# A two-layer diffusion step on one core: the fourth feed-forward row by seven products, three output splits placed later, and a projection's weights made ahead of modulation tiles

## The chip, the core and the metric

The program runs on one core of a Trainium2 chip. The metric is the device time of one execution in microseconds (us). Three runs of the kernel before gave 1493.72, 1493.82 and 1495.14 us, so the median is 1493.82 us.

The core's engines run side by side, each through its own list of instructions in order: TensorE (PE in the profile; PEld is its weight load), VectorE (DVE), ScalarE (ACT), GpSimd (POOL) and SyncE (SP), which in this kernel issues nearly all DMAs. An instruction that waits holds up everything behind it on its engine.

## The reference, cut to what matters

Two groups of tokens go through the same two trunk layers: 512 latent tokens and 128 prompt tokens. They are held together as T = 640 columns of feature-major tiles (128 features by 640 tokens, eight tiles for the model width 1024).

```python
for l in range(DEPTH):                                    # DEPTH = 2
    sh1, sc1, g1, sh2, sc2, g2 = ada_modulation(cond, w_mod[l], b_mod[l])
    h = modulate(rms_norm(x, norm_mix[l]), sh1, sc1)
    # l = 0: 8 latent-attention (MLA) heads and 8 neighbourhood heads, joined, then @ w_out_a
    # l = 1: grouped-query attention, then @ w_out_c
    x = x + g1 * mixer(h)
    h = modulate(rms_norm(x, norm_ffn[l]), sh2, sc2)
    x = x + g2 * swiglu(h, w_ffn_in[l], w_ffn_out[l])
def swiglu(h, w_in, w_out):
    gate, up = jnp.split(h @ w_in, 2, axis=-1)            # 1024 -> 2 x 2816
    return (jax.nn.silu(gate) * up) @ w_out
```

Everything is in 32-bit floats, and the products keep that precision by splitting each operand into a high and a low part and taking three matmuls (high x high, high x low, low x high).

## The kernel before

**Splits.** `rsplit(src, name)` (lines 458 to 463) writes the high part of a 128 x 640 tile with an ACT copy (L461) and the low part with a DVE subtraction (L462). `unit(src, n, name)` (lines 168 to 175) does the same for a 128 x 1024 tile of weights: a load into one of three `raw` buffers (SP, L165), an ACT copy (L173) and a subtraction (L174, on DVE, or on POOL for a few) into one of three `w` buffers of the pool `wp`.

**The order.** The framework takes the program's text as priority, simulates the engines with a cost model and writes out a fixed order for every engine; buffers are given out in that order too, so a load waits until the instructions on the buffer's last content have ended. `after(inst, fn)` binds the instructions of `fn` that run on the engine of `inst` behind `inst`; it adds no wait across engines.

**Latent attention of layer 0.** Eight heads in a loop; `exps[h, j]` is the ACT exponential of head h and query block j (L965, tile `mp`), and POOL then scales the block by the inverse sum (L384). A head's tail (five groups of four transposes `mt`, their splits `mts`, and the products `mo` with the values) is woven into the next head's scores. Beside it, the eight finished output tiles are split for the projection that follows: `oN[0..3]` from the neighbourhood heads, done before the loop, and `oM[0..3]`, one for each pair of latent heads. The splits of `oN` are bound behind `exps[h, 3]` of heads 0, 2, 4 and 5. Those of `oM[0..2]` stand after the loop in the text and are bound to nothing, so the planner takes them up as gaps appear. `oM[3]` needs the last head. All these splits lie in eight pairs of ring buffers.

**Projection of layer 0** (`mixer_out`, name `oa`). For each of eight output rows n it takes the weights `un(n)` (tile `oaw`n) and 24 matmuls for each half of the columns, in the order oN0 to oN3, oM0 to oM3; rows 0 and 1 leave their last part (oM3) to the end of row 1. `evac` adds the result to x (`xr`, L324), which `x_again` has loaded afresh behind a DVE copy out of `oMs3l` (L1672). Between the rows stands `beside(n - 1)`: with the counts (1, 1, 1, 1, 0, 0, 0) it loads one 128 x 1024 tile `wm` of the modulation weights (L1648) and takes two DVE products with accumulation (L1630, tile `junk`). The weights are asked for by the first matmul that needs them, so in the text `beside(n - 1)` stands ahead of `un(n)`; with `early` set, `un(n)` stands ahead. The projection of layer 1 has `early` set.

**Feed-forward of layer 0** (`ffn`, l = 0). Each of the 22 rows (`fb`) of 128 hidden features takes a tile of gate weights and a tile of up weights. The first `FEW[0]` = 4 rows are plain: 2 tiles x 2 halves x 8 steps x 3 matmuls. The rows after them take seven products over half-size blocks instead of eight (`seven`, lines 1169 to 1186, in the manner of Strassen and Winograd): DVE forms sums of quarters of the two weight tiles (`s13`, `s24`: L1179 to L1184), three 1024-wide tiles wX, wY, wZ are split by `split` (L1370 on ACT, L1371 on DVE), and the 512-wide wW by L1176 and L1177. On the other side stand sums of the normalised tokens (`h01D`, `h01N`, `h01C`, `h01E`), made by `add_up` during the plain rows 0 and 1. After each row, `hidden` splits the result (`hd`) and sends it out to DRAM; `step("fb", fb)` may take modulation tiles.

`split` counts its calls in `turn[0]` and gives its results to the pool `fp` and `wp` in turn. The same counter goes on into the second half, the projection back to 1024 features: `wout` adds one for each of its calls and, for a call with a single tile, takes the buffers of `rawp` and `wp` when the count is odd, and those of the pool `fo` (one raw buffer, two `w` buffers) when it is even. `rawp` is shared with the loads of modulation tiles. The tiles are `wo_`; the first figure is the output row, the second the first of its blocks.

```python
x, pend = mixer_out(wOA, oMs + oNs, [4, 5, 6, 7, 0, 1, 2, 3], x_again, mods[0], "oa", nxt, op[-1],
                    before(op[1], op[5], (1, 1, 1, 1, 0, 0, 0)))
early = len(tiles) > 1 or turn[0] % 2          # in wout
```

Of the kernel before, what the change touches and what calls it, by code (L numbers as in the profile page):

```python
# [51 lines left out]
def body(ctx, tc, xT, vecs, crow, wm0, wm0g1, wm0g, wm1, wA, wNV, wNA, wMK, wMV, wOA, wGQ, wGK, wGV, wOC,  # L52
# [53 lines left out]
    def f(ap):  # L106
        return ap.bitcast(F32)
# [19 lines left out]
    def named(prefix, pieces):  # L127
        return {f"{prefix}{i}": piece for i, piece in enumerate(pieces)}
# [17 lines left out]
    mods = [main.tile([P, 48, 2], F32, name=f"mods{l}") for l in range(2)]  # L146
# [30 lines left out]
    def after(inst, fn):  # L177
        if inst is None:
            return fn()
        with tc.issue_after(inst.ins):  # L180
            return fn()

    def mm3(ps, a, b, h, l, st, sp, **k):
        PE.matmul(ps, a, h, start=st, stop=False, **k)
        PE.matmul(ps, a, l, start=False, stop=False, **k)
        PE.matmul(ps, b, h, start=False, stop=sp, **k)
# [271 lines left out]
    def rsplit(src, name):  # L458
        h = ring.tile([P, T], F32R, tag="hh", name=name + "h")
        l = ring.tile([P, T], F32R, tag="hl", name=name + "l")  # L460
        S.activation(h, src, AF.Copy)  # L461
        V.tensor_tensor(l, src, f(h), ALU.subtract)  # L462
        return h, l
# [30 lines left out]
    x = []  # L494
# [335 lines left out]
    def k_tiles(r, p):  # L830
        return odd_keys[p % 2] if r else even_keys
# [26 lines left out]
    mqs, exps = {}, {}  # L858
# [19 lines left out]
    tail, oN = {}, []  # L878
# [4 lines left out]
    for h in range(8):  # L883
        p, r = divmod(h, 2)
# [68 lines left out]
    def mla_scores(h, pts):  # L953
        r = h % 2
        ll = tiny.tile([P, 4], F32, tag="ll", bufs=4, name=f"ml{h}")

        def piece(j):
            qh, ql = mqs[h]
            pss = bank2(f"ms{h}_{j}")
            kh, kl = [t[0] for t in k_tiles(r, h // 2)]  # L960
            scores(pss, (qh[:, P * j:P * j + P], ql[:, P * j:P * j + P]), kh, kl)
            nm = tiny.tile([P, 1], F32, tag="nm", name=f"mn{h}_{j}")
            V.tensor_reduce(nm, pss[:, :, :HT], AX.XY, ALU.max, negate=True)
            pt = cp.tile([P, T], F32, tag="mp", bufs=8, name=f"mp{h}_{j}")
            exps[h, j] = S.activation(halves(pt), pss[:, :, :HT], AF.Exp, bias=nm, accum_out=ll[:, j:j + 1])  # L965
            softmax_tail(pt, ll[:, j:j + 1], f"mr{h}_{j}", T)
            pts.append(pt)
        return [lambda j=j: piece(j) for j in range(4)]
# [31 lines left out]
    tail, oM, oNs = {}, [], []  # L1000
# [4 lines left out]
    for h in range(8):  # L1005
        p, r = divmod(h, 2)
        if r == 0:
            oM.append(cp.tile([P, T], F32, tag="om", bufs=4, name=f"oM{p}"))
            pfirst, psecond = prompt_pair([mv[5][:, 2 * p + i, :] for i in range(2)], oM[p], cp, f"mpp{p}",
                                         bank)  # L1010
        pts = []
        sc = mla_scores(h, pts)
        qh, ql = mqs[h]
        pieces = named("s", sc)
        pieces["sp"] = pfirst(r, lambda pss, qh=qh, ql=ql, ks=k_tiles(r, p): mm3(pss, qh[:, NS:T], ql[:, NS:T], ks[0][1], ks[1][1], True, True))
        if h == 0:
            pieces.update({f"b{i}": lambda i=i: mv_late(i) for i in BESIDE})
        if h < 7:
            pieces.update(named("q", mla_q(h + 1)))
            if r == 1:  # L1020
                pieces.update(k_pieces(p + 1, qbank))
        sequence(MLA_ORDER[r], {**pieces, **late, **{k: v for k, v in tail.items() if k not in ("v3", "v4")}})
        late = {"w" + k[1]: tail[k] for k in ("v3", "v4") if k in tail}

        def out_m(ps, h=h, p=p, r=r):
            half_sum(((oM[p][64 * r:64 * r + 64, 0:NS], 0, NS),), ps, NS, cp, f"mhs{h}")
        tail = values(h, pts, lambda b, th, tl, h=h: [(mv[b][:, h, :], th), (mv[b][:, h, :], tl)], cp, "m", out_m)
        if r == 1:
            tail.update(psecond)
        if h in (0, 2, 4, 5):  # L1030
            oNs.append(after(exps[h, 3], lambda: rsplit(oN[len(oNs)], f"oNs{len(oNs)}")))
    oMs = [rsplit(oM[p], f"oMs{p}") for p in range(3)]
    sequence("w3 t0 w4 t1 t2 v0 t3 pt v1 t4 v2 v3 v4 pv", {**tail, **late})
    oMs.append(rsplit(oM[3], "oMs3"))
    mkgs(0, 1)
# [13 lines left out]
    def mixer_out(wsrc, os_, order, xin, ml, name, nxt, pre, beside=None, early=False, hold=None):  # L1049

        nrm = Norm(name + "n", D)
        oh, ol = [o[0] for o in os_], [o[1] for o in os_]
        x = []
        ks = [(k, k) for k in order]
        if True:
            def wunit(n):
                get = lazy(lambda: after(hold if n == 2 else None, lambda: unit(wsrc[n], 1024, f"{name}w{n}")))
                return lambda w0: (get(), w0)

            def evac(n, c, ps):  # L1060
                if c == 0:
                    x.append(xin(n))
                residual(x[n], x[n], ps, ml, G1, n, c)
                nrm.add(x[n], c)

            def half(ps, un, c, ks, first=True, last=True):
                two_halves([ps], [un], ks, oh, ol, c, first=first, last=last)

            held = []
            uns = [wunit(n) for n in range(KT)]  # L1070
            for n in range(KT):
                un = uns[n]
                if beside and n >= 1:
                    if early:
                        un(0)
                    beside(n - 1)
                if n < 2:
                    ps = pair(f"{name}{n}")
                    for c in range(2):
                        half(ps, un, c, ks[:-1], last=False)  # L1080
                    held.append((ps, un))
                    if n == 1:
                        for i, (ps, un) in enumerate(held):
                            for c in range(2):
                                half(ps, un, c, ks[-1:], first=False)
                                evac(i, c, ps[c])
                        held = []
                elif n < 5:
                    ps = pair(f"{name}{n}")
                    for c in range(2):  # L1090
                        half(ps, un, c, ks)
                        evac(n, c, ps[c])
                else:
                    ps = pair(f"{name}{n}") if n < 7 else [bank(f"{name}{n}{c}") for c in range(2)]
                    half(ps, un, 0, ks)
                    evac(n, 0, ps[0])
                    held.append((n, ps, un))
            pre()
            for j in range(KT - 2):
                for n, ps, un in held:  # L1100
                    half(ps, un, 1, ks[j:j + 1], first=j == 0, last=False)
                if j >= 1:
                    nxt(x, nrm, 0, (j - 1,))
            for i, (n, ps, un) in enumerate(held):
                half(ps, un, 1, ks[-2:], first=False)
                evac(n, 1, ps[1])
                nxt(x, nrm, 0, (5 + i,))
        return x, lambda: nxt(x, nrm, 1, range(KT))
# [11 lines left out]
                box["m"].make(c, nrm.rs, k)  # L1120
        return box, nxt

    FEW = 4, 3
    STAY = 3
    FIRST, SECOND = FO_ORDER[:9], FO_ORDER[9:]

# [233 lines left out]
    def ffn(l, x, pend, hm, nxt, side, opened):  # L1360
# [80 lines left out]
        step = None  # L1441
        few = FEW[l]
        for fb in range(few):
# [226 lines left out]
    def x_again(n):  # L1670
# [5 lines left out]
    op = ffn_open(0)  # L1676
    box, nxt = next_mod("h01", gs[0][1], mods[0], SH2, op[7])
    side, before = mod_side([(0, wm0g, G2)] + [(1, wm1[j:j + 8], j) for j in (SH1, SC1, G1, SH2, SC2)],
                            lambda kind, i: int(i > 4 and i % 3 > 0 or i == 21) if kind == "fb" else
                            (0, 1, 1, 1, 2, 2, 2, 2, 3, 3, 3, 3, 3, 2, 2, 2)[i])  # L1680
    x, pend = mixer_out(wOA, oMs + oNs, [4, 5, 6, 7, 0, 1, 2, 3], x_again, mods[0], "oa", nxt, op[-1], before(op[1], op[5], (1, 1, 1, 1, 0, 0, 0)))
    box2, nxt = next_mod("h10", gs[1][0], mods[1], SH1)
    x, pend = ffn(0, x, pend, box["m"], nxt, side, op)

# [187 lines left out]
    for h in range(8):  # L1872
# [4 lines left out]
        if h < 7:  # L1877
# [10 lines left out]
    op = ffn_open(1)  # L1888
    box, nxt = next_mod("h11", gs[1][1], mods[1], SH2, op[7])
    _, before = mod_side([(1, wm1[G2:], G2)], None)  # L1890
    x, pend = mixer_out(wOC, oGs, list(range(8)), lambda n, x=x: x[n], mods[1], "oc", nxt, op[-1],
                        before(op[5], op[5], (2, 1, 1, 2, 1, 1, 0)), True, hold=gexp[7, 3])
# [11 lines left out]
    x, pend = ffn(1, x, pend, box["m"], final, lambda pool: lambda kind, i: None, op)  # L1904
# [158 lines left out]
```

## Time and profile before

| what | value |
|---|---|
| median of three runs | 1493.82 us |
| the profiled execution's own time | 1495.92 us |
| its span, first to last instruction | 1494.1 us |
| TensorE busy | 1448.7 us, 97% |
| VectorE busy | 1235.9 us, 83% |
| ScalarE busy | 785.7 us, 53% |
| GpSimd busy | 178.0 us, 12% |
| mean granted TensorE clock | 0.994 |

The span starts at 0. In the profile of before, head 5's last exponential starts at about 295.3 us and head 7's at 318.2 us; the projection `oa` runs from 319 to about 384 us (its first matmuls are mixed into the last head's tail); the plain feed-forward rows run from about 390 to 446 us, the rows by seven products to 670 us, and the projection back to about 824 us. The rest is layer 1.

A row of the timeline gives the start, the duration, the engine, the line, the operation, the tile written and the tiles read, and in brackets how long the engine had been idle before it and what ended that idle time. A duration on PE is that of one pipelined matmul or a run of them ("x12"); the pace shows in the distance between starts. SPq rows are DMA requests.

### The profile page before, as it was taken

The numbers are of one execution on the slowest core, as the hardware profiler recorded it, in microseconds if no ns is written. First come the engines' busy times: TensorE is split into PE (matmuls) and PEld (weight loads), VectorE is DVE, ScalarE is ACT, GpSimd is POOL, SyncE is SP. The second block draws the span as 40 slices with busy tenths as digits, with TensorE's granted clock in tenths as the row PEclk, the third lists the DMA queues.
The fourth block names the chain that finished last, engine by engine and source line by source line (L and its number), as shares of the span: only waits on it lengthen the run. The fifth ranks groups of instructions, "written<-read, shape, count | busy, mean of one in ns | idle before, by whom it ended". The sixth has DMA issues, their size and how long they took to land.

```text
span 1494.1 us, 25843 instructions
## 1 busy us (share of the span) xinstructions
PE 1448.7 (97%) x9766; PEld 1392.5 (93%) x9766; DVE 1235.9 (83%) x2378; ACT 785.7 (53%) x1542; POOL 178.0 (12%) x272
## 2 busy tenths in 40 slices
PE   6999999999999999999999999999999999999997
PEld 4989978889899999999999999989899999999996
DVE  5877778877878888955998888888899989989976
ACT  5446677763745555541222656672665565555443
POOL 0046635420000000000000122220100000000000
PEclk9999999999999999999999999999999999999999
DMA  9643341025154554559765301115154555548561
GB/s 372 207 151 123 114 145 44 15 81 188 42 208 167 166 166 166 163 181 345 234 215 189 96 27 36 37 40 193 57 170 171 190 175 190 174 151 294 184 260 71
DMA packets 79636, 231.48 MB, mean 155 GB/s; under 512 B 8856, under 2 KB 13240, under 8 KB 79128
## 3 DMA queue, kind: packets, MB, share of 16 engines
q1 hardware_dynamic: 77152, 225.43, 44.2%
q10 hardware_dynamic: 1944, 3.48, 0.7%
q8 instruction: 76, 1.25, 0.3%
q0 software_dynamic: 416, 0.93, 0.2%
q14 instruction: 48, 0.39, 0.1%
HBM read 193.15 MB, written 36.66 MB: 154 GB/s over the span
## 4 chain that ended last, share of the span: by engine, by line
PE 77%; DVE 10%; ACT 6%; DMA 4%; issue 2%; POOL 0%; DVEq 0%; ACTq 0%; SPq 0%; POOLq 0%
PE fg L64 19%; PE fd L64 9%; PE fgo L64 5%; PE fu L64 4%; PE gq L64 3%; PE fdo L64 3%; PE fo L64 2%; DVE junk L1630 2%; PE gs L64 2%; PE go L64 2%; PE nk L64 2%; PE nq L64 2%; PE fuo L64 1%; PE gt L68 1%; PE mod L64 1%
## 5 line engine op out<-in xcount | busy, mean ns | idle before, releaser
L1630 DVE SCALAR_TENSOR_TENSOR junk<-wm,cb 128x1024 bf16<-128x1024 f32 x88 | 107.3, 1219 | 1.8 <-DMA wm<-in_wm 1.2
L64 PE MATMUL gq<-h10h,wgq 128*128 128x320 f32 x256 | 65.8, 316 | 0.0
L261 POOL TENSOR_SCALAR h10h<-h10t,gs,mods 128x320 fp32r<-128x320 f32 x4 | 3.1, 786 | 438.2 <-DVE h10t L255 435.9
L1370 ACT ACTIVATE wY<-s 128x1024 fp32r<-128x1024 f32 x37 | 39.2, 1060 | 27.7 <-PE fg L64 24.0
L1898 POOL TENSOR_TENSOR xr<-xw,fn1rs 128x320 f32<-128x320 f32 x2 | 1.7, 866 | 416.9 <-ACT fn1rs L229 416.9
L1370 ACT ACTIVATE wZ<-s 128x1024 fp32r<-128x1024 f32 x37 | 39.1, 1057 | 18.8 <-PE fd L64 16.5
L1479 DVE TENSOR_TENSOR sg<-up,sg 128x640 f32<-128x640 f32 x37 | 30.5, 823 | 20.7 <-ACT sg L1478 19.6
L1371 DVE TENSOR_TENSOR wZ<-s,wZ 128x1024 fp32r<-128x1024 f32 x37 | 45.2, 1222 | 2.8 <-ACT wZ L1370 0.2
L64 PEld LDWEIGHTS gq<-h10h,wgq 128*128 128x128 f32 x256 | 44.9, 189 | 0.6
L1371 DVE TENSOR_TENSOR wY<-s,wY 128x1024 fp32r<-128x1024 f32 x37 | 45.1, 1219 | 0.3
L1478 ACT ACTIVATE sg<-fg 128x320 f32<-128x320 f32 x37 | 16.2, 438 | 48.7 <-PE fg L64 48.7
L64 PE MATMUL fg<-h01q,wgu 128*128 128x320 f32 x192 | 40.3, 316 | 0.9 <-ACT h01q L298 0.5
L1500 ACT ACTIVATE p<-fd 128x320 f32<-128x320 f32 x37 | 16.2, 438 | 46.9 <-PE fd L64 46.9
L64 PE MATMUL gq<-h10l,wgq 128*128 128x320 f32 x128 | 39.4, 308 | 0.0
L1835 ACT ACTIVATE gp<-gs,gb,rq 128x640 f32<-128x640 f32 (+1 forms) x40 | 31.8, 796 | 13.2 <-DVE gb L1834 11.8
L64 PE MATMUL fg<-h11q,wX 128*128 128x320 f32 x228 | 36.7, 309 | 0.0
L64 PE MATMUL fu<-h11q,wX 128*128 128x320 f32 x228 | 36.6, 309 | 0.0
L64 PE MATMUL fd<-h11q,wZ 128*128 128x320 f32 x228 | 36.6, 309 | 0.0
L64 PE MATMUL fg<-h11E,wW 128*128 128x320 f32 x228 | 36.5, 309 | 0.0
L64 PE MATMUL fg<-h11N,wZ 128*128 128x320 f32 x228 | 36.5, 309 | 0.0
L64 PE MATMUL fd<-h11D,wY 128*128 128x320 f32 x228 | 36.4, 308 | 0.0
L64 PE MATMUL fg<-h11C,wY 128*128 128x320 f32 x228 | 36.4, 308 | 0.0
(3425 smaller groups left out, 5331.1 us busy)
## 6 DMA issues: line engine op xcount, KB each, us to landing
wm<-in_wm SPq DMA_DIRECT2D x48, 512.0 KB, 4.3
mraw<-in_wm SPq DMA_DIRECT2D x8, 1024.0 KB, 13.2
mraw<-in_wm SPq DMA_DIRECT2D x16, 512.0 KB, 4.0
wmv<-in_wm0g SPq DMA_DIRECT2D x8, 512.0 KB, 4.3
wm<-in_wm0g SPq DMA_DIRECT2D x8, 512.0 KB, 3.5
ruo<-in_wFO SPq DMA_DIRECT2D x8, 512.0 KB, 4.7
rgo<-in_wFO SPq DMA_DIRECT2D x8, 512.0 KB, 5.9
x<-in_xT SPq DMA_DIRECT2D x8, 320.0 KB, 5.4
```

The lines of the kernel that those rows point to most:

```text
L64: cls.last = nc.tensor.matmul(*a, **k)
L68: cls.last = nc.tensor.transpose(*a, **k)
L261: G.tensor_scalar(h[:, c0:c1], t, self.gsl[:, k, 0:1], self.ml[:, self.sh + k, 0:1], ALU.mult, ALU.add)
L1370: S.activation(h, src, AF.Copy)
L1371: V.tensor_tensor(w_, src, f(h), ALU.subtract)
L1478: last = S.activation(sg[:, 0:HT], g[:, :HT], AF.Silu, scale=-1.0)
L1479: V.tensor_tensor(sg, up, sg, ALU.mult)
L1500: S.activation(p5, b5[:, :HT], AF.Copy)
L1630: V.scalar_tensor_tensor(junk, raw, 1.0, cb[:, c, :], ALU.mult, ALU.mult, accum_out=mods[l][:, j0 + i, c:c + 1])
L1835: gexp[h, j] = S.activation(dst, src, AF.Exp, bias=nb, scale=rq[:, j:j + 1], accum_out=ll[:, j:j + 1])
L1898: G.tensor_tensor(x[k][:, c0:c1], root[1][k], nrm.rs[:, c0:c1], ALU.mult)
```

## The change

Three edits:

1. `FEW = 3, 3`: the fourth row of layer 0's feed-forward (fb = 3) goes by seven products.
2. The split of `oN[3]` is bound behind `exps[7, 2]` instead of `exps[5, 3]`, and the splits of `oM[0]`, `oM[1]` and `oM[2]`, which were bound to nothing, behind `exps[7, 3]`.
3. The projection of layer 0 gets `early = True`: for rows 1 and up, `un(n)` stands ahead of `beside(n - 1)` in the text.

Since row 3 now calls `split` three times, `turn[0]` is 57 instead of 54 when the second half of the feed-forward begins, so every single-tile `wout` of layer 0 changes sides between the two sets of buffers.

```diff
@@ -1027,9 +1027,10 @@
         if r == 1:
             tail.update(psecond)
-        if h in (0, 2, 4, 5):
+        if h in (0, 2, 4):
             oNs.append(after(exps[h, 3], lambda: rsplit(oN[len(oNs)], f"oNs{len(oNs)}")))
-    oMs = [rsplit(oM[p], f"oMs{p}") for p in range(3)]
+    oNs.append(after(exps[7, 2], lambda: rsplit(oN[3], "oNs3")))
+    oMs = [after(exps[7, 3], lambda: rsplit(oM[p], f"oMs{p}")) for p in range(3)]
     sequence("w3 t0 w4 t1 t2 v0 t3 pt v1 t4 v2 v3 v4 pv", {**tail, **late})
@@ -1120,7 +1121,7 @@
-    FEW = 4, 3
+    FEW = 3, 3
@@ -1678,7 +1679,7 @@
-    x, pend = mixer_out(wOA, oMs + oNs, [4, 5, 6, 7, 0, 1, 2, 3], x_again, mods[0], "oa", nxt, op[-1], before(op[1], op[5], (1, 1, 1, 1, 0, 0, 0)))
+    x, pend = mixer_out(wOA, oMs + oNs, [4, 5, 6, 7, 0, 1, 2, 3], x_again, mods[0], "oa", nxt, op[-1], before(op[1], op[5], (1, 1, 1, 1, 0, 0, 0)), True)
```

## The prediction, made before the result was known

> **What bounds the kernel now.** I read the busy shares and the chain of work that ended last, then the stages by windows, then the waits of TensorE in the stages that the diff touches.
>
> ```profile
> PE 1448.7 (97%) x9766; PEld 1392.5 (93%) x9766; DVE 1235.9 (83%) x2378; ACT 785.7 (53%) x1542; POOL 178.0 (12%) x272
> ...
> PE 77%; DVE 10%; ACT 6%; DMA 4%; issue 2%; POOL 0%; DVEq 0%; ACTq 0%; SPq 0%; POOLq 0%
> ```
>
> TensorE is the bound, so a gain is a matmul less or one of its few idle gaps closed. The windows (span; then busy PE, PEld, DVE, ACT, POOL) say where gaps are:
>
> ```profile
> 296.00:312.00 16.00, 14.25 (x92) 12.57 (x93) 15.52 (x30) 12.33 (x30) 6.63 (x8) 1.00 0.03 6
> ...
> 320.00:330.00 10.00, 9.94 (x65) 8.68 (x64) 5.92 (x13) 5.49 (x11) 0.69 (x2) 1.00 0.27 107
> ...
> 340.00:350.00 10.00, 9.20 (x62) 8.71 (x61) 9.76 (x20) 4.58 (x9) 0.00 (x0) 1.00 0.57 207
> ...
> 420.00:430.00 10.00, 10.00 (x70) 10.00 (x69) 3.12 (x4) 2.65 (x4) 0.00 (x0) 1.00 0.77 295
> ...
> 480.00:660.00 180.00, 180.00 (x1230) 180.00 (x1229) 151.63 (x220) 92.08 (x144) 0.00 (x0) 1.00 0.49 161
> ```
>
> TensorE idles 1.75 us in the latent heads 5 to 7, where DVE is full, 0.80 in the projection, and nothing in the long run of seven-product rows; two more waits, 0.94 and 0.9, are shown below. The sum is made against the profiled execution (1495.92 us, span 1494.1, so 1.8 outside it), which stands 2.1 above the median of the three runs, 1493.82. I apply the difference to the median. About 0.2%, 3.0 us, is what a measurement here can tell from no change.
>
> **Row 3 by seven products.** A plain row has 2 x 2 x 8 x 3 = 96 matmuls, a seven-product row 7 x 4 x 3 = 84. Twelve take 448.22 - 446.46 = 1.76 us:
>
> ```profile
> 434.76 2.18 PE L64 MATMUL fu_3a<-h01q,wgu 128*128 128x320 f32 x13 [0.94 <-DVE wgu L174]
> ...
> 446.46 1.92 PE L64 MATMUL fg<-h01q,wX 128*128 128x320 f32 x12
> 448.22 1.92 PE L64 MATMUL fd<-h01D,wY 128*128 128x320 f32 x12
> ```
>
> So -1.76 us, with TensorE never idle in the rows that follow. The first row shows a stall of 0.94 us in the old row 3: TensorE waits for its up weights. Their raw tile is asked for at 417.30, but their `w` buffer frees only when row 2 ends, so ACT splits at 431.14 and DVE at 433.49:
>
> ```profile
> 403.77 0.33 SPq L165 DMA_DIRECT2D wgu_30r<-in_wFI  x1
> ...
> 417.30 0.33 SPq L165 DMA_DIRECT2D wgu_31r<-in_wFI  x1
> ...
> wgu_31r<-in_wFI SPq DMA_DIRECT2D x1, 512.0 KB, 6.9
> ...
> 431.14 1.05 ACT L173 ACTIVATE wgu<-wgu_31r 128x1024 fp32r<-128x1024 f32 x1
> ...
> 433.49 1.22 DVE L174 TENSOR_TENSOR wgu<-wgu_31r,wgu 128x1024 fp32r<-128x1024 f32 x1
> ```
>
> The new row inherits these two requests (up tile at 403.77, gate tile at 417.30), but its three splits alternate between `fp` and `wp`, where buffers of row 0 are free. Are its sums in time? The old row 4 shows the chain from a landed gate tile:
>
> ```profile
> 428.50 0.63 ACT L1176 ACTIVATE wW<-wg_4r 128x512 fp32r<-128x512 f32 x1 [0.20 <-DMA wg_4r<-in_wFI]
> ...
> 435.36 1.22 DVE L1371 TENSOR_TENSOR wY<-s,wY 128x1024 fp32r<-128x1024 f32 x1
> ...
> 436.50 1.22 DVE L1371 TENSOR_TENSOR wZ<-s,wZ 128x1024 fp32r<-128x1024 f32 x1
> ```
>
> From 428.5 to the end of wY's low half, 436.6, are 8.1 us. The gate tile lands at 417.30 + 6.9 = 424.2, so wY is ready by 432.3 and wZ by 433.4. Row 2 ends about 431.4 (446.46 less 96 matmuls, 14.1, and the stall), so TensorE wants wY one product later, 433.2, and wZ after a second, 434.9. That covers wY by 0.9 us, and by more where DVE is free, as it is for 6.9 us of 420 to 430. So the 0.94 goes too. DVE's added work is one more split of 1.22, one of half the width, four half-width sums (an estimate: 0.6 each, half a split) and about 1.4 on results, 5.7 us in all. Those 6.9 us hide it, and ACT's, which idles 7.35 there; uncovered it would cost up to 5.7. Bounds of the wait: -0.94 if it goes, +3.4 if the gate tile comes where row 4's came (wY at 436.6 against 433.2). I take -0.94, since the request is the inherited one. Late next would be wY, by the margin above; the rows after it only move up.
>
> **The output splits.** Where they run now, with POOL's scaling and TensorE's waits:
>
> ```profile
> 296.87 1.31 DVE L462 TENSOR_TENSOR oNs3l<-oN,oNs3h 128x640 fp32r<-128x640 f32 x1
> ...
> 299.90 0.81 DVE L462 TENSOR_TENSOR oMs0l<-oM,oMs0h 128x640 fp32r<-128x640 f32 x1
> ...
> 306.60 1.40 DVE L462 TENSOR_TENSOR oMs1l<-oM,oMs1h 128x640 fp32r<-128x640 f32 x1 [0.24 <-ACT oMs1h L461]
> ...
> 317.87 0.81 DVE L462 TENSOR_TENSOR oMs2l<-oM,oMs2h 128x640 fp32r<-128x640 f32 x1
> ...
> 305.84 0.73 ACT L461 ACTIVATE oMs1h<-oM 128x640 fp32r<-128x640 f32 x1
> ...
> 311.26 0.50 PE L64 MATMUL mo<-mts_4l,mv 128*128 128x512 f32 x1 [1.16 <-DVE mts_4l L391]
> ...
> 318.12 1.22 POOL L384 TENSOR_SCALAR mp<-mp,mr_2r 128x640 f32<-128x640 f32 x1 [1.65 <-DVE mr_2r L383]
> ...
> 319.52 0.80 POOL L384 TENSOR_SCALAR mp<-mp,mr_3r 128x640 f32<-128x640 f32 x1 [0.17 <-DVE mr_3r L383]
> ```
>
> The first three leave 296 to 312, taking 3.5 us from a DVE that is busy 15.52 of 16. TensorE's longest wait, 1.16 us, is for a DVE split that stands behind oMs1l (1.40); the chain of waits runs through it. Bounds: 0 to -1.75 (all idle time there). I take -1.16, the wait with a removed instruction on its chain; whatever is left waits for DVE still.
>
> They come back behind the exponentials of head 7, from 317 to 323: four times 0.74 on ACT and 0.8 on DVE, of which oMs2 was there already. ACT is busy 5.49 and DVE 5.92 of 10 in 320 to 330, and TensorE has matmuls of `oa` to fill in, as it does from 319 on. What stands behind them are the last head's splits, its output, oMs3 and the x loads. Bounds: 0, to four times 0.74, about 3.0, if every ACT copy delays that chain and nothing fills. I take +0.5, nearer to the row of 320 to 330 with TensorE at 9.94.
>
> **Weights first in the projection.**
>
> ```profile
> 310.49 0.33 SPq L165 DMA_DIRECT2D oaw5r<-in_wOA  x1
> ...
> 330.75 0.33 SPq L1648 DMA_DIRECT2D wm<-in_wm0g  x1
> ...
> 349.27 0.33 SPq L165 DMA_DIRECT2D oaw6r<-in_wOA  x1
> ...
> 339.17 1.06 ACT L173 ACTIVATE oaw<-oaw3r 128x1024 fp32r<-128x1024 f32 x1 [9.30 <-PE oa0b L64]
> ...
> 346.25 1.22 DVE L1630 SCALAR_TENSOR_TENSOR junk<-wm,cbo 128x1024 bf16<-128x1024 f32 x1
> ...
> 347.98 1.22 DVE L174 TENSOR_TENSOR oaw<-oaw3r,oaw 128x1024 fp32r<-128x1024 f32 x1
> ...
> 346.89 0.31 PE L64 MATMUL oa3a<-oNs0h,oaw 128*128 128x320 f32 x1
> ...
> 348.22 0.39 PE L64 MATMUL oa4b<-oNs0h,oaw 128*128 128x320 f32 x1 [0.29 <-DVE xr L324]
> ...
> 349.26 0.41 PE L64 MATMUL oa3a<-oNs0h,oaw 128*128 128x320 f32 x1 [0.51 <-DVE oaw L174]
> ```
>
> On SP hardly anything moves: rows 0 to 5 are asked for by 310.49, ahead of the first `wm`, and row 6 waits for row 3's split. What moves is DVE's rank. Row 3's high half is there at 340.2, its low half starts at 347.98 behind the `junk` pair of the third tile; with `un(3)` first it passes that pair, 2.4 us, and ends near 346.8, as TensorE arrives (346.89). The tile's two products run behind it, where DVE is less busy; nothing waits for their sums before the feed-forward's second half. Bounds 0 and -0.80 (both gaps), +0.3 if a load of x falls behind. I take -0.80.
>
> **The flipped buffers.** With `turn[0]` odd instead of even, the first weights of rows 4 to 7 leave the raw buffers that they share with `wm`, and the second, needed 30 matmuls (4.4 us) later, go there.
>
> ```profile
> PE fo_6a L64 <- DVE wo L1547: 0.9, 1, 0.9
> ...
> 716.69 0.82 DVE L1547 TENSOR_TENSOR wo<-wo_60r,wo 128x640 fp32r<-128x640 f32 x1
> ...
> 670.34 0.43 SPq L1541 DMA_DIRECT2D wo_13r<-in_wFO  x1
> ...
> 676.99 0.96 DVE L1547 TENSOR_TENSOR wo<-wo_13r,wo 128x768 fp32r<-128x768 f32 x1 [3.72 <-ACT wo L1546]
> ...
> 678.96 0.31 PE L64 MATMUL fo_0a<-hr_0h,wo 128*128 128x320 f32 x1
> ```
>
> The one wait of the stage, 0.9 us, is for such a first tile. Against this, row 0's tile now takes the single `fo` buffer, which row 1's took: asked for at 670.34, split by 677.95, and TensorE wants it at 678.96. Bounds -0.9 to +1.0; I take -0.9.
>
> Sum: -1.76 - 0.94 - 1.16 + 0.5 - 0.80 - 0.9 = -5.06, and 1493.82 - 5.06 = 1488.8 us. With this case's bounds it lies between 1486.8 and 1490.8.
>
> **The rivals.**
> - *Priority moves nothing*: the requests stay, DVE keeps its order, and the flip moves no deadline. Without -0.80 and -0.9: 1490.5, still faster. For it: the requests that are already early. Against: the `junk` pair ahead of row 3's split.
> - *The tail gives back the gain*: the last head's copies and splits wait behind the four pairs on ACT and DVE, and nothing fills: +3.0 for +0.5, 1491.3, within 0.2% of before. For it: they all come after 317, ahead of the last chain. Against: ACT and DVE are half idle from 320 on.
> - *The lock in the tail*: two splits (0.81 each) placed ahead of head 7's last scaling on POOL make it 1.6 us later, +1.6 for +0.5: 1489.9. For it: splits beside POOL work took 1.31 and 1.40. Against: only the block at 319.52 is left then.
> - *The fourth row's weights come late* (slower): the gate tile's request slips down SP's line. Forecast 417.30, wanted by 418.2. If it is issued after 423.3, the wait eats the whole sum; after 426.3 the kernel is over 0.2% slower. If it came 15 us later, TensorE would wait 14.1: 1502.9. For it: this request already stood 13.5 us behind the one before it (403.77), held by a buffer. Against: buffers are given out in turn, and the tile takes an existing place.
>
> One rule of the Trainium skill stands behind the lock. "SBUF — State Buffer", section "Who interferes with whom", says that a VectorE instruction with two SBUF inputs and a GpSimd instruction that reads SBUF exclude each other, the second blocking until the first ends. The trace agrees: 1.31 and 1.40 us beside POOL work against 0.81 alone, and POOL's 1.22 beside oMs2l against 0.80. By that rule the sum would be this rival's, 1489.9; without it, 1488.8.
>
> **How the numbers follow.** The sum as it stands 0.42; the lock 0.07; priority moves nothing 0.17; the tail 0.17; late weights 0.17, of which 0.02 within 0.2%. So faster 0.66, same 0.19, slower 0.15. The predicted time is 1488.8. The range takes in the first four cases, with the bounds of their costs, and the smaller part of the last: 1486.6 to 1495.5.
>
> **What would show it.** Right: 84 matmuls in row 3; no wait of TensorE for wgu or wX, wY, wZ between 425 and 450; none of 1 us for mts in heads 5 to 7; row 3's low half of `oaw` ahead of the third `junk` pair; `wo_60` no longer waited for. Wrong: a wait on s13 or wY in row 3, TensorE idle after head 7, x loads that hold rows 0 to 2 of `oa`, or a new gap in a later stage whose fixed order came out differently.

## The result, and the profile after

The changed kernel takes 1490.19 us (median of 15 runs, 1487.04 to 1492.56) where the kernel before takes 1494.11 (15 runs, 1491.67 to 1498.65). The medians are 3.9 us apart. The ratio is 0.9964, 95% interval 0.9955 to 0.9973: 5.4 us less, with 4.0 to 6.7 in the interval. The forecast was 5.06 less, 1488.8 us; the measured median is 1.4 us above that. The sum came near; as will be seen, its terms did not.

The page of the changed kernel, busy times and the chain of work that ended last. TensorE is still the bound and now carries 83% of the chain, 77% before; the chain's share on DVE fell from 10 to 7%:

```profile
PE 1443.6 (97%) x9754; PEld 1388.5 (93%) x9754; DVE 1238.1 (83%) x2386; ACT 788.4 (53%) x1547; POOL 179.1 (12%) x272
...
PE 83%; DVE 7%; ACT 5%; DMA 2%; issue 2%; POOL 0%; DVEq 0%; ACTq 0%; POOLq 0%; SPq 0%
```

The windows of the changed kernel (span; then busy PE, PEld, DVE, ACT, POOL, the granted clock, DMA), the same ones as were shown of before, and one more:

```profile
296.00:312.00 16.00, 15.19 (x99) 13.28 (x98) 13.97 (x30) 12.78 (x28) 7.11 (x9) 1.00 0.11 34
320.00:330.00 10.00, 10.00 (x68) 9.36 (x67) 6.74 (x19) 4.07 (x8) 0.14 (x1) 1.00 0.26 107
340.00:350.00 10.00, 10.00 (x70) 10.00 (x69) 9.58 (x19) 2.46 (x4) 0.00 (x0) 1.00 0.69 234
420.00:430.00 10.00, 9.87 (x68) 9.60 (x66) 8.73 (x13) 4.65 (x7) 0.00 (x0) 1.00 0.58 212
430.00:440.00 10.00, 6.77 (x46) 6.77 (x47) 9.69 (x14) 6.07 (x10) 0.00 (x0) 1.00 0.51 173
```

The heads went from 14.25 of 16 to 15.19, the tail from 9.94 of 10 to 10.00, the projection from 9.20 to 10.00: the gaps that the forecast meant to close are closed. But 430 to 440 holds a new one, 3.2 us. The list of waits names it, with two smaller ones that the first profile of before did not have:

```profile
PE fg L64 <- ACT p L1499: 3.4, 1, 3.4
...
PE mk L64 <- POOL wm L174: 1.3, 1, 1.3
...
PE fg L64 <- DVE g L1511: 0.9, 1, 0.9
```

The timeline of the changed kernel around the first row (ACT, DVE and TensorE, in that order; the bracket is the idle time before an instruction and what ended it):

```profile
428.95 1.06 ACT L1371 ACTIVATE wY<-s 128x1024 fp32r<-128x1024 f32 x1 [1.95 <-DVE s L1181]
429.92 0.42 ACT L1463 ACTIVATE sg<-fg 128x320 f32<-128x320 f32 x1
430.24 1.05 ACT L1371 ACTIVATE wX<-wu_4r 128x1024 fp32r<-128x1024 f32 x1
431.18 1.05 ACT L1371 ACTIVATE wZ<-s 128x1024 fp32r<-128x1024 f32 x1
432.13 0.72 ACT L1431 ACTIVATE hd_0h<-sg 128x640 fp32r<-128x640 f32 x1
432.75 0.42 ACT L1499 ACTIVATE p<-fg 128x320 f32<-128x320 f32 x1
...
427.03 1.23 DVE L1372 TENSOR_TENSOR wZ<-s,wZ 128x1024 fp32r<-128x1024 f32 x1
428.18 0.68 DVE L1181 TENSOR_TENSOR s<-wu_4r,wg_4r 128x512 f32<-128x512 f32 x1
...
427.94 1.92 PE L64 MATMUL fd<-h01D,wY 128*128 128x320 f32 x12
433.23 2.02 PE L64 MATMUL fg<-h01N,wZ 128*128 128x320 f32 x12 [3.37 <-ACT p L1499]
```

Row 3's last weights, wZ, are ready at 428.26, ahead of TensorE. What is late is the copy `p` of its first product out of the bank `fg`: until it has run, the product `N` may not be added in that bank. The product ended about 428.1, but on ACT the copy stands behind five instructions for other rows: three splits of row 4, and `sg` and `hd` of row 2. The first of them, a split of row 4, is preceded by 1.95 us in which ACT waits for row 4's sums.

Stage by stage. Each length is taken between starts of matmuls as the traces have them: the last `mk` (the latent heads' keys), the last `oa0a` (row 0 of the projection), the first `fu_1a` (plain row 1), the first `fo_0a` (the projection back) and the first `fn0p` (the sums for the norm behind it). Of before, for instance, the first length is 338.4 - 291.9 = 46.5. "Again" is a second profiled execution of the same kernel; the other columns are the experiments below.

| stage (us) | before | again | splits | weights | both | row | turn | changed | again | mended | mended, even |
|---|---|---|---|---|---|---|---|---|---|---|---|
| heads and tail, `mk` to `oa0a` | 46.5 | 46.5 | 45.0 | 46.5 | 45.1 | 46.4 | 46.4 | 45.1 | 45.1 | 45.1 | 45.1 |
| projection, to `fu_1a` | 63.6 | 63.6 | 65.2 | 62.3 | 62.3 | 63.7 | 63.6 | 62.3 | 62.3 | 62.3 | 62.3 |
| rows, to `fo_0a` | 264.3 | 263.9 | 266.8 | 264.5 | 264.1 | 262.5 | 263.4 | 264.6 | 262.9 | 261.0 | 261.0 |
| second half, to `fn0p` | 151.3 | 149.9 | 150.2 | 150.1 | 150.1 | 148.3 | 149.5 | 149.4 | 149.7 | 149.2 | 148.3 |

### The profile page after: what moved, and what is told of

It reads as the page before. It is cut to its first block, busy times and chain, and to the rows that moved or that the text cites. A ratio compares the mean times of both kernels' runs of the same rounds, so it can differ in the third digit from the quotient of the medians.

```text
span 1489.9 us, 25823 instructions
## 1 busy us (share of the span) xinstructions
PE 1443.6 (97%) x9754; PEld 1388.5 (93%) x9754; DVE 1238.1 (83%) x2386; ACT 788.4 (53%) x1547; POOL 179.1 (12%) x272
## 3 DMA queue, kind: packets, MB, share of 16 engines
q8 instruction: 76, 1.25, 0.3%
## 4 chain that ended last, share of the span: by engine, by line
PE 83%; DVE 7%; ACT 5%; DMA 2%; issue 2%; POOL 0%; DVEq 0%; ACTq 0%; POOLq 0%; SPq 0%
PE fg L64 18%; PE fd L64 9%; PE fgo L64 5%; PE fo L64 5%; PE fu L64 4%; PE gq L64 3%; PE fdo L64 3%; PE gs L64 2%; PE go L64 2%; PE nk L64 2%; PE nq L64 2%; PE fuo L64 1%; PE gt L68 1%; PE mod L64 1%; PE ms L64 1%
## 5 line engine op out<-in xcount | busy, mean ns | idle before, releaser
L1372 DVE TENSOR_TENSOR wZ<-s,wZ 128x1024 fp32r<-128x1024 f32 x38 | 46.4, 1220 | 2.4
L1501 ACT ACTIVATE p<-fd 128x320 f32<-128x320 f32 x38 | 16.6, 438 | 45.6 <-PE fd L64 45.6
L64 PE MATMUL fg<-h01N,wZ 128*128 128x320 f32 x228 | 36.6, 309 | 3.4 <-ACT p L1499 3.4
L64 PEld LDWEIGHTS fg<-h01N,wZ 128*128 128x128 f32 x228 | 34.2, 188 | 3.6 <-ACT p L1499 3.6
L64 PE MATMUL fg<-h01E,wW 128*128 128x320 f32 x228 | 36.6, 310 | 0.9 <-DVE g L1511 0.9
L64 PE MATMUL fg<-h01q,wX 128*128 128x320 f32 x228 | 36.7, 309 | 0.0
L64 PE MATMUL fd<-h01q,wZ 128*128 128x320 f32 x228 | 36.6, 309 | 0.0
```

Of the source, the lines that this page charges most:

```text
L64: cls.last = nc.tensor.matmul(*a, **k)
L1372: V.tensor_tensor(w_, src, f(h), ALU.subtract)
L1501: S.activation(p5, b5[:, :HT], AF.Copy)
```

## The experiments

**The splits alone.** The theory after the two traces (the ledger): each edit gains what its stage became shorter, but the row gives nearly all of its gain back in the wait for `p`. The rival is the forecast's own list of terms.

```diff
-        if h in (0, 2, 4, 5):
+        if h in (0, 2, 4):
...
-    oMs = [rsplit(oM[p], f"oMs{p}") for p in range(3)]
+    oNs.append(after(exps[7, 2], lambda: rsplit(oN[3], "oNs3")))
+    oMs = [after(exps[7, 3], lambda: rsplit(oM[p], f"oMs{p}")) for p in range(3)]
```

> The kernel before with the four output splits moved behind head 7's exponentials, and nothing else. Ledger theory (from the changed kernel's trace: from the end of the latent keys' products to the end of the projection's row 0 TensorE was 1.4 us shorter): 1.2 to 1.5 us faster than before, the wait of 1.2 us for mts_4l gone, TensorE busy about 15.2 of 16 us in the four-microsecond stretches that answer to 296 to 312, and no idle time after head 7. Forecast's sum: 0.66 faster, with half a microsecond lost in the tail. Rival, the tail gives back: 1.2 gained, 3.0 lost, so 1.8 slower.

Measured: slower, ratio 1.0014 (1.0004 to 1.0024). The heads gain 1.5 us as the ledger has it, and nothing is lost in the tail; no theory had seen what comes after. The waits of this kernel, and DVE's order in the projection:

```profile
PE oa3a L64 <- DVE oaw L174: 2.1, 1, 2.1
PE fu_3a L64 <- DVE wgu L174: 1.8, 1, 1.8
```

```profile
342.25 1.22 DVE L1631 SCALAR_TENSOR_TENSOR junk<-wm,cbo 128x1024 bf16<-128x1024 f32 x1
...
344.38 1.22 DVE L1631 SCALAR_TENSOR_TENSOR junk<-wm,cbo 128x1024 bf16<-128x1024 f32 x1
...
345.92 1.23 DVE L174 TENSOR_TENSOR oaw<-oaw3r,oaw 128x1024 fp32r<-128x1024 f32 x1
```

TensorE comes to row 3 of the projection earlier, but the low half of its weights still stands behind the third pair of `junk` products: 0.51 us of wait became 2.1. The old row 3's wait for `wgu` grew too, to 1.8 from 0.94 and 0.5 in the two profiles of before; that this has the same reason is argued, not shown. Here, a gain ahead of a queue whose order stayed was paid back at the next thing that queue held. (The rows' 266.8 also hold a stretch at granted clock 0.83, 430 to 440. Against the second profile of before, the rows are 2.8 us longer and the wait for `wgu` 1.25; so some 1.5 us, an estimate, go with the slower clock in this one execution.)

**One kind of split at a time.** First `oNs3` alone, then `oMs0` to `oMs2` alone:

```diff
-        if h in (0, 2, 4, 5):
+        if h in (0, 2, 4):
...
+    oNs.append(after(exps[7, 2], lambda: rsplit(oN[3], "oNs3")))
```

> The kernel before with oNs3 alone moved behind head 7's third exponential. Forecast's reading (the wait for mts_4l stands behind oMs1l): the wait of 1.2 us stays, since oMs1 is where it was. Rival (any 1.4 us taken off a full DVE does it): it goes or falls below 0.5.

> The kernel before with oMs0 to oMs2 alone bound behind head 7's last exponential. Forecast's reading: the wait for mts_4l goes, and the stage from the keys' end to the end of the projection's first row is 45.1 us, as with all four moved. Rival: half of it stays. The wait of row 3 of the projection for its weights is 0.5 if it hangs on oNs3's place, 2.1 if it hangs on the three.

One execution each, 1496.74 and 1496.77 us, beside one of before at 1498.62; single times decide nothing here. The wait for `mts_4l` is gone in both, against what the forecast's reading expected of the first; the heads take 45.1 and 45.6 us; `oaw` of row 3 is waited for 2.1 us in both. With `oNs3` alone moved, the trace shows that the others went along:

```profile
315.21 0.83 DVE L462 TENSOR_TENSOR oNs3l<-oN,oNs3h 128x640 fp32r<-128x640 f32 x1
...
317.10 1.24 DVE L462 TENSOR_TENSOR oMs0l<-oM,oMs0h 128x640 fp32r<-128x640 f32 x1 [0.21 <-ACT oMs0h L461]
...
318.94 0.80 DVE L462 TENSOR_TENSOR oMs1l<-oM,oMs1h 128x640 fp32r<-128x640 f32 x1
```

So this run does not separate the two readings: `oMs1l` left the heads there too, although nothing bound it. Both are in accord with the forecast's reading that the wait stood behind `oMs1l`; neither proves it against "any 1.4 us less". `oNs3` adds 0.5 us to the three.

**The weights alone.**

```diff
-..."oa", nxt, op[-1], before(op[1], op[5], (1, 1, 1, 1, 0, 0, 0)))
+..."oa", nxt, op[-1], before(op[1], op[5], (1, 1, 1, 1, 0, 0, 0)), True)
```

> The kernel before with the projection's weights asked for ahead of the modulation tiles, and nothing else. Ledger theory (in the changed kernel this stage is 1.3 us shorter): 0.8 to 1.3 us faster, row 3's low half ahead of the third pair of junk products, no wait of TensorE in rows 3 and 4. Rival, priority moves nothing: within 0.2 us, the waits 0.51 and 0.29 still there.

Ratio 0.9989 (0.9979 to 0.9998), 1.6 us less. The projection is 1.3 us shorter, and its two waits are gone.

**Both of them, without the fourth row** (the changed kernel with `FEW = 4, 3`).

> The changed kernel with four plain rows as before: the splits and the early weights without the fourth row by seven products, buffer sides as before. Ledger theory: 1.4 (heads and tail) plus 1.3 (projection) faster, 2.7 in all, some 1 more if the waits of the second half go too; the old wait for wgu_31's split is there again with 0.9 to 1.8 us. If the two edits only undo each other, as the splits alone were 2 us slower and the weights alone 1.6 faster: within 0.5 us of before.

Ratio 0.9985 (0.9976 to 0.9994), 2.2 us less. The stages show both gains in full, 1.4 and 1.3. Splits and weights do not undo each other: the 1.6 us that the projection lost with the splits alone are gone when the weights come early. The edits are therefore not additive one by one (+2.1 for the splits, -1.6 for the weights), and the pair is the unit to be priced.

**The fourth row alone**, with the buffer count put back to even.

```diff
-    FEW = 4, 3
+    FEW = 3, 3
...
+        turn[0] += 1
         pss, ws = {}, {}
```

> The kernel before with the fourth row by seven products, the buffer count put back to even ahead of the second half, and nothing else. Ledger theory: 84 matmuls for 96 (-1.76) and no wait for wgu (-0.94), but a wait of about 3.4 us for the ACT copy p of row 3, since row 4's splits stand ahead of it on ACT: within 1 us of before. Forecast's theory: no such wait, 2.7 us faster. Third theory, the wait came from the other edits' shift of time: no wait here, 2.7 faster, and it is not the row's own.

Ratio 0.9978 (0.9968 to 0.9988), 3.3 us less: neither the ledger's "within 1 us" nor without a wait. The rows took 262.5 us, and the wait for `p` was 1.3 us, not 3.4. First the wait and then the DMA of row 3's gate tile in this kernel (512 KB; last, the median us from issue to landing), then that DMA in the changed kernel's first profile:

```profile
PE fg L64 <- ACT p L1498: 1.3, 1, 1.3
```

```profile
wg_3r<-in_wFI SPq DMA_DIRECT2D x1, 512.0 KB, 6.4
```

```profile
wg_3r<-in_wFI SPq DMA_DIRECT2D x1, 512.0 KB, 8.5
```

The tile landed 2.1 us later in the changed kernel's profile, and the wait was 2.1 us longer. With the buffer count even, the second half took 148.3 us here.

**The changed kernel once more**, to see whether that is a coincidence. No edit.

> The changed kernel itself, profiled a second time. If the 3.4 us wait of row 3 for its copy p is fixed by the order on ACT alone, it is 3.4 again; if it grows with the landing of row 3's gate tile (8.5 us after its request in the first profile, 6.4 in the run of the fourth row alone, where the wait was 1.3), it is 1.3 us plus what the tile takes above 6.4 us.

1489.43 us, ratio 0.9970 (0.9960 to 0.9981). In this profile, the waits and the DMA of the gate tile:

```profile
PE fg L64 <- ACT p L1499: 1.4, 1, 1.4
...
PE fg L64 <- DVE g L1511: 1.2, 1, 1.2
```

```profile
wg_3r<-in_wFI SPq DMA_DIRECT2D x1, 512.0 KB, 6.5
```

1.3 + (6.5 - 6.4) = 1.4, as expected. So in these three profiles the landing of the gate tile sets the size of the wait, 1.3 us and more. That the order of the instructions makes it is for the next run to show.

**The order mended**, in the changed kernel: row 4's splits on ACT are bound behind row 3's copy `p`, and its sums and splits on DVE behind row 2's last product `sg`.

```diff
-                V.tensor_tensor(sg[:, c0:c1], pu[c][:, :HT], sg[:, c0:c1], ALU.mult)
+                sums = V.tensor_tensor(sg[:, c0:c1], pu[c][:, :HT], sg[:, c0:c1], ALU.mult)
...
-            wX, wW, wY, wZ = seven(ru, rg, f"{l}_{fb}", fp, split)
+            parts = lambda: seven(ru, rg, f"{l}_{fb}", fp, split)
+            wX, wW, wY, wZ = after(copied, lambda: after(sums, parts)) if l == 0 and fb == few + 1 else parts()
...
-            S.activation(p1, g[:, :HT], AF.Copy)
+            copied = S.activation(p1, g[:, :HT], AF.Copy)
```

> The changed kernel, with the splits and sums of row 4 bound behind row 3's copy p on ACT and behind row 2's last product on DVE. If the order on ACT is the cause of the 3.4 us wait, it goes, wholly or but for some 0.5 us, and the kernel is 2.9 to 3.4 us faster than the changed one, about 8.5 faster than before. If the copy p is late for another reason (its data, a buffer), the wait stays and the time is that of the changed kernel; if row 4's own weights are then late, a wait of 1 to 3 us for wX or wY of row 4 takes its place.

1488.27 us, ratio 0.9958 (0.9942 to 0.9974). The timeline of the mended kernel, ACT and TensorE:

```profile
428.89 0.74 ACT L1431 ACTIVATE hd_0h<-sg 128x640 fp32r<-128x640 f32 x1 [0.60 <-DVE sg L1465]
429.76 0.44 ACT L1500 ACTIVATE p<-fg 128x320 f32<-128x320 f32 x1
430.10 1.05 ACT L1371 ACTIVATE wX<-wu_4r 128x1024 fp32r<-128x1024 f32 x1
...
429.56 1.92 PE L64 MATMUL fd<-h01D,wY 128*128 128x320 f32 x12
431.32 1.92 PE L64 MATMUL fg<-h01N,wZ 128*128 128x320 f32 x12
```

The copy runs as soon as its product is done, the wait is gone, and nothing of row 4 is late: the rows take 261.0 us against 264.6 and 262.9. The order is the cause, on ACT and DVE together: on DVE, row 2's product `sg`, which `hd` ahead of the copy needs, starts at 431.36 in the changed kernel, behind row 4's sums, and at 428.37 in the mended one. The edit moves both orders at once, so the share of ACT's alone is not shown. The time fell by less than expected, 1.9 us by the medians and 0.9 by the ratios instead of 2.9 to 3.4, with intervals that overlap; a wait that is 1.4 us in other executions, and not 3.4, would leave no more.

**The flip of buffers.** In the kernel before alone (`turn[0] += 1` ahead of the second half), and taken back in the mended kernel (the same line there).

> The kernel before with the count of splits made odd ahead of the second half of layer 0's feed-forward, and nothing else. Forecast's step: the wait of 0.9 us of fo_6a for its weights goes, so 0.9 faster; row 0's late tile may wait up to 1.0 in its place. Rival: the wait does not hang on the buffer's side, since the run of the fourth row alone lost it with the side kept; then within 0.3 us of before, with the wait in place or another like it. If the 1.4 us wait of fn0p for fn0acc also goes, it hangs on the order on DVE that any edit redraws.

> The mended kernel (row 4's splits and sums behind row 3's copy p) with the buffer sides of the second half as before the change. If the flip is worth 0.9 us, this is 0.9 slower than the mended one, with a wait of fo_6a; if the waits of that half hang on the redrawn order only, within 0.5 us of it.

Alone it does nothing: ratio 1.0002 (0.9990 to 1.0015), and TensorE still waits 0.9 us for the same tile:

```profile
PE fo_6a L64 <- DVE wo L1547: 0.9, 1, 0.9
```

The mended kernel with the sides as before takes 1485.28 us (1483.76 to 1486.43), ratio 0.9938 (0.9925 to 0.9950), an interval that lies below both of the changed kernel's. So the flip is not worth 0.9 us. Together with the fourth row it costs something: against the mended kernel the second half is 0.9 us shorter and the median 3.0, though the intervals of the two ratios just overlap. One difference is the wait for `g` at the end of the last row (0.9 and 1.2 in the changed kernel, 0.7 in the mended one, none here). DVE, of the changed kernel:

```profile
662.69 1.22 DVE L1631 SCALAR_TENSOR_TENSOR junk<-wm,cb 128x1024 bf16<-128x1024 f32 x1
...
663.83 0.48 DVE L1511 TENSOR_TENSOR g<-fg,p 128x320 f32<-128x320 f32 x1
```

A `junk` product, its tile of `wm` late from the shared raw buffers, stands ahead of `g`. With the sides as before (the mended, even kernel) that pair is done by then:

```profile
657.89 1.22 DVE L1633 SCALAR_TENSOR_TENSOR junk<-wm,cb 128x1024 bf16<-128x1024 f32 x1
...
659.55 0.49 DVE L1512 TENSOR_TENSOR g<-fg,p 128x320 f32<-128x320 f32 x1
```

But the flip is not the wait's only way in. With the fourth row by seven products, three profiles with the flip have it and two without it (this one and the row alone) do not. With four plain rows and no flip, five of seven profiles have it too, at 0.2 to 0.8 us, and the flip alone has none. Of the kernel with `oNs3` alone moved:

```profile
PE fg L64 <- DVE g L1511: 0.8, 1, 0.8
```

There DVE has two splits of `wo` ahead of `g`, not a `junk` product. The kernel before has the same two splits there, with a wait of 0.2 us in one profile and none in the other, so the order alone does not fix the wait. That the flip acts through the raw buffers is argued.

**The kernel before once more.** No edit; one execution, 1493.33 us.

> The kernel before, profiled a second time. If the 1.4 us wait of fn0p belongs to the kernel, it is there again. If it was that one execution's (its tile wgk1's neighbour wgk0r landed late, and DVE's order is the same in three kernels that have no such wait), it is gone, and the wait of fo_6a, 0.9, and the one for mts_4l, 1.2, stay, since they hang on the order.

The waits of `fo_6a` and `mts_4l` are there again, that of `fn0p` is not:

```profile
PE mk L64 <- POOL wm L174: 1.3, 1, 1.3
PE mo L64 <- DVE mts_4l L391: 1.2, 1, 1.2
...
PE fo_6a L64 <- DVE wo L1547: 0.9, 1, 0.9
```

So 1.4 us of the difference between the two first profiles were one execution's and no one's edit, and the wait of `mk`, new in the changed kernel's first profile, belongs to before as well.

## Why the prediction was right in its sum and wrong in its terms

- **Row 3's matmuls, -1.76: right.** TensorE has 9754 matmuls for 9766, and where nothing disturbs the row (mended) the rows take 261.0 us against 263.4 to 264.5 in the five columns with four plain rows at full clock: 2.4 to 3.5 less, where the row's two terms made 2.70.
- **Row 3's stall, -0.94: the wait went, a longer one came.** The request was inherited as forecast: 417.30 less the 4.6 us by which the kernel was ahead is 412.7, and that is where it stands. The tile took 8.5 us to land, not 6.9, and the weights were still in time. The step that failed is "Late next would be wY": late next was the copy `p`. I had followed the weights on both engines, but not the copy of the first product, which shares ACT with the next row's splits and waits behind sums that row 3 does not need. I named DVE's cover in microseconds and gave ACT's idle time, 7.35, as its cover. But in the changed kernel 1.95 us of ACT's idle time are a split waiting for its data, with the copy behind it: idle time like that covers nothing. Measured: +1.4 in one profile and +3.4 in another for -0.94; the stage of the rows, +0.3 between the first profiles of the two kernels and -1.0 between the second, for -2.70.
- **Splits, -1.16 and +0.5 in the tail: the sign right, the tail mis-sized.** Heads and tail gave -1.4; the tail cost nothing, TensorE being full from 320 to 330. On their own, however, they make the kernel slower, by the projection's weights and in the rows. I had summed the three edits as if each stood alone, which came out because the kernel has all of them.
- **Weights, -0.80: right in mechanism, too small.** Row 3's low half passes the third `junk` pair (342.60 in the changed kernel, 347.98 before), both waits are gone, and the stage is 1.3 us shorter. Of that, the windows from 338 to 402 show 0.80 as idle time (62.32 us of TensorE work before, 63.12 after), which is the forecast. The other 0.5 lies in the distances between starts. Of before, a matmul ahead of both waits and one behind them:

```profile
347.62 0.31 PE L64 MATMUL oa4a<-oNs0l,oaw 128*128 128x320 f32 x1
...
349.51 0.31 PE L64 MATMUL oa3a<-oNs1h,oaw 128*128 128x320 f32 x1
```

  From the first to the second are four steps, 1.89 us, with both waits in them. Undisturbed matmuls of this form start 0.147 us apart, so four steps would take 0.59: the two waits cost 1.30 us, not 0.80. The bracket counts from the end of a matmul that is shown as 0.31 us long, although the next one could have started after 0.147; and the matmul behind each of the two waits is followed after 0.22 and 0.25 us. The forecast took the brackets for the price. The wait for `p` shows the same: 1.31 us in the bracket with the row alone, where the rows take 1.5 us more than in the mended kernels.
- **The flip, -0.9: wrong.** I took the raw buffer for the cause. The profile had the answer: the raw tile's high half was split at 711.25 and its low half only at 716.69, behind row 5's result, which TensorE has to finish first. The rows of before:

```profile
714.33 0.55 DVE L324 SCALAR_TENSOR_TENSOR xr<-fo,mods,xr 128x320 f32<-128x320 f32 x1 [1.30 <-PE fo L64]
714.80 1.22 DVE L1630 SCALAR_TENSOR_TENSOR junk<-wm,cb 128x1024 bf16<-128x1024 f32 x1
...
716.09 0.68 DVE L324 SCALAR_TENSOR_TENSOR xr<-fo,mods,xr 128x192 f32<-128x192 f32 x2
```

  It is its place in DVE's order again, and the fourth row, not the flip, moved it: in the changed kernel the split runs at 707.69, ahead of row 5's result at 710.84, and in the kernel with the row alone the wait is gone with the sides kept. Why the order there came out otherwise I can't say. Against the second profile of before, the second half as a whole gave -0.2 to -0.5.
- **The sum.** By the second profiles of both kernels the stages give -1.4, -1.3, -1.0 and -0.2, 3.9 us, and the stretch behind them takes 1.7 us more in the changed kernel (last section); the ratios over all executions give 5.4 and 4.5. Splits and weights without the row gave 2.2 and the row with the sides kept 3.3, 5.5 in all, but the changed kernel has the sides flipped, so that is not its sum. A forecast of 5.06 came near because terms too small (0.7 in the heads, 0.5 in the projection) made up for half of the terms too large (1.7 in the row, 0.7 in the flip). That is luck. The bounds of the sum, 1486.8 to 1490.8, do not follow from the bounds of its terms either: these give 1487.7 with all at their best (-6.15) and 1499.8 with all at their worst (+5.94).
- **The rivals.** *Late weights* was the right place and the wrong operand; its price, at 1.4 to 3.4 us, stayed below the point from which it decides. *The lock in the tail* happened and cost nothing. In the changed kernel POOL's last small block, 0.37 us alone, took 1.52 beside two splits:

```profile
309.85 0.37 POOL L384 TENSOR_SCALAR mpp3p<-mpp3p,mpp3r0r 128x128 f32<-128x128 f32 x1
...
318.62 1.52 POOL L384 TENSOR_SCALAR mpp3p<-mpp3p,mpp3r1r 128x128 f32<-128x128 f32 x1 [1.44 <-DVE mpp3r1r L383]
...
318.45 0.80 DVE L462 TENSOR_TENSOR oMs1l<-oM,oMs1h 128x640 fp32r<-128x640 f32 x1
319.17 0.81 DVE L462 TENSOR_TENSOR oMs2l<-oM,oMs2h 128x640 fp32r<-128x640 f32 x1
```

  By the rule of the Trainium skill ("SBUF — State Buffer", section "Who interferes with whom") the one that comes second waits for the whole of the other; the trace agrees, since the block ends 0.16 us after the second split and not before. But TensorE had the projection's first rows to fill in. *Priority moves nothing* is refuted by the weights alone, *the tail gives back* by the tail at 10.00 of 10.

## What to carry to other kernels

When an operation is sped up, list not only its own operands but everything that its banks and buffers wait for, and read on each engine which instruction of another row stands ahead of it and what that one waits for: here, binding the next row's work behind two instructions removed a wait of 1.4 to 3.4 us, and the row's edit saves 1.76 us of matmuls. Price a wait of TensorE by the distance between starts, not by the bracket. An edit that shortens a stage ahead of a queue in fixed order must be priced with the next thing that queue delivers: the splits alone made the kernel slower, and with the weights faster. Before a wait of about a microsecond is put into a sum, take a second profile of the same kernel: some of them belong to one execution.

## What was not expected of the hardware

The same load in the same place took 6.4 to 8.5 us to land (`wg_3r`; 8.5 and 6.5 in the two executions of the changed kernel, four 512 KB tiles and one of 1 MB being asked for within 7 us), and TensorE's wait followed it one for one.

TensorE's granted clock drops for a few us in the middle of work, and not in the same places in two executions of one kernel: around 200 us in the first profile of before (0.50 from 201 to 207) and not in the second; near 875 us in both of the changed kernel (0.50 from 876 to 878) and in no other of the thirteen profiles. Of the changed kernel's first profile:

```profile
870.00:875.00 5.00, 4.51 (x34) 3.99 (x32) 4.91 (x11) 2.46 (x7) 1.74 (x2) 1.00 0.24 75
875.00:880.00 5.00, 5.00 (x28) 4.96 (x27) 3.35 (x8) 2.75 (x7) 0.58 (x1) 0.66 0.08 33
```

From `fn0p` to the last `gs`, the stretch that holds it, took 180.7 us in both, 179.0 in both profiles of before: 1.7 us, as much as the fourth row's matmuls. How many of the unprofiled executions have such drops is not known, but they differ: the three fastest of the changed kernel's 15 (1487.04 to 1487.40) had mean granted clocks of 0.997 to 0.999, the three slowest (1491.83 to 1492.56) 0.994 to 0.995. The Trainium skill ("TensorE: Matmul & The Clock Gate", section "What's actually happening") has the clock fall after an idle window of about 3.4 us; here TensorE was busy 4.51 of the 5 us ahead of it, so the trace does not agree that so long an idle time is needed, and no run shows what is. The drop around 200 us goes with the loss of a wait: all seven profiles without it show `mk` waiting 1.3 us for POOL's split of `wm`, and the six with it do not.
